# Products over partitions of an attention: from SBUF tiles into a PSUM bank of the logits, with a scan that restarts by a maximum

## The chip, the cores and the metric

The kernel runs on one core of one Trainium2 chip. The metric is the device time of one execution in microseconds (us); lower is better. The core has TensorE (PE in the profile, its weight loads PEld), VectorE (DVE), ScalarE (ACT), GpSimd (POOL), SyncE (SP, which here only issues transfers) and 16 DMA engines. Each engine runs its instructions in the order in which they stand in its queue.

## The reference

One layer of a hybrid encoder on `x` of 2048 x 1024 in float32: RMS norm, one input projection, three mixers side by side (a short gated convolution A, a convolution module B of width 31, and stick-breaking attention C with 8 heads of 64), one output projection, and a squared-ReLU MLP of width 4096, each with its residual, and a final RMS norm. The change is in the attention:

```python
z = jnp.einsum("bhqd,bhkd->bhqk", qb, kb) * scale
mask = s_idx < t_idx
log_beta = jax.nn.log_sigmoid(z)
log_1m = jnp.where(mask, log_beta - z, 0.0)
suffix = lax.cumsum(log_1m, axis=3, reverse=True) - log_1m
a = jnp.where(mask, jnp.exp(log_beta + suffix), 0.0)
out = jnp.einsum("bhqk,bhkd->bhqd", a, vb)
```

So the weight of key s for query t is sigmoid(z) times the product of (1 - sigmoid(z')) over all keys s' between s and t. The kernel forms that product directly.

## The kernel before

Keys lie on the 128 partitions, the 512 queries of a block in the free dimension. A key's partition p and step j say which key it is: of J keys that lie next to each other in time, each of the J steps takes one, so that a partition owns J successive keys. The product over later keys then falls into two: over the steps of the same partition, which is elementwise between tiles (`R`), and over the partitions behind it, which is the part that changes (`a_cross_a`).

`attention` runs over pairs (head h, query block i). For each pair `a_pass1` makes three diagonal steps (`a_diag`: logits `ps_z`, two sigmoids `om` and `A0` on ScalarE, masks on POOL at L537, products) and, for i > 0, 4i late steps. It carries the products over steps: for the diagonal in `om[:, hi2]` (L561 for 256 queries, L580 for the other 256), for the late steps in `R` (L603). The product over the 128 partitions goes so: each 32 x 32 block is transposed into a tile `T` of 16 groups x 33 columns (L564, L581 the two halves of the diagonal; L609 the late one); a scan from the right multiplies along the free dimension (L617), where the 33rd column of a group, set to 0 by POOL (L563, L608) and met by a 1 in the constant `d1`, begins each group anew; the products of whole groups of 32 partitions are chained in a small tile `C` (L620 or L622 the start, L625 three products of 32 x 16, L629 the total `tot`, which seeds the late part); the last product multiplies `T` by `C` (L631). `a_pass2` of the same pair, which runs interleaved with `a_pass1` of the next one, transposes the result back into a bank `ps_q` (L649), multiplies the `A0` tiles by it (L652, L659), splits each into a high and a low part (L88 on ScalarE, L90 on POOL) and multiplies by V (L697 to L706).

All of that runs beside a TensorE that is fed by other work: query block 0 beside the second half of the input projections (`p_half(1)`) and convolution B (L452 on VectorE); query blocks 1 to 3 beside the output projection and the FFN (`block`) of time blocks 0 to 2. `weave` hands out the attention steps in proportion to the main work. Instructions are then put in order by a scheduler that plays the program through with its own durations; on each engine the planned order is fixed. PSUM has eight banks: in the first part three for the projections (`ps_p`), one for convolution B, two for logits (`z`), one each for `ps_q` and `ps_o`; from the FFN on three for `ps_x`, `ps_u`, `ps_y`, three for logits, and the same two. Buffers of a tag are used in turn; whoever takes one waits for the last reader of the tile before. `om` has two buffers, `R` one in the first part and two later.

In the FFN, `fl` (L927) is the low part of an activation that TensorE multiplies next, and also frees the bank `ps_u`. L975 scales the eight tiles `acc` near the start of each block. In the first two blocks VectorE also splits the weights (`w<-wraw,w`, L90).

Of the kernel before, what the change touches and what calls it, by code (L numbers as in the profile page):

```python
# [15 lines left out]
P = 128  # L16
# [3 lines left out]
TB = 512  # L20
# [48 lines left out]
class Trunk:  # L69
# [126 lines left out]
    def attention_consts(self, ctx):  # L196
        nc = self.nc
        c = ctx.enter_context(self.tc.tile_pool(name="aconsts", bufs=1))
        self.d1 = c.tile([P, 16, 33], F32, name="d1")
        nc.vector.memset(self.d1, 0.0)  # L200
        nc.vector.memset(self.d1[:, :, 32:33], 1.0)


    def p_pools(self, ctx):
# [337 lines left out]
    def a_pass1(self, g):  # L542
        nc, pool, i = self.nc, self.at, g["i"]
        ab = self.ab
        lo, hi2 = slice(0, 256), slice(256, 512)

        def new(name, bufs, shape=(P, TB), dt=F32):
            return pool.tile(list(shape), dt, name=name, tag=name, bufs=bufs)

        if i:  # L550
            g["Kl"] = pool.tile([P, self.kmax], F32R, name="Kl", tag="Kl", bufs=self.ab["Kl"])
            for rows, kq in self.kq_halves(g["h"]):
                to = g["Kl"][rows, : TB * i].rearrange("c (j q) -> c j q", j=2)
                self.load_r(to, kq[:, 0, :, : TB * i // 2])
        A0 = g["A0"] = []

        k2 = [g["Kd"][:, 0:P], g["Kd"][:, 256 : 256 + P]]
        z = self.a_z(g, [(k2[1], lo, lo), (k2[0], lo, hi2)])
        t, om = self.a_diag(z, 0)
        nc.gpsimd.tensor_tensor(t[:, hi2], t[:, hi2], om[:, lo], op=ALU.mult)  # L560
        nc.vector.tensor_tensor(om[:, hi2], om[:, lo], om[:, hi2], op=ALU.mult)  # L561
        T = pool.tile([P, 16, 33], F32, name="T", tag="T1", bufs=ab["T1"])
        nc.gpsimd.memset(T[:, :, 32:33], 0.0)  # L563
        nc.vector.transpose(T[:, 0:8, 0:32], om[:, hi2])  # L564
        A0.append(t)
        yield 1

        k4 = self.every(g["Kd"], 4)
        z = self.a_z(g, [(k4[3], hi2, lo), (k4[2], hi2, hi2)])
        t, om = self.a_diag(z, 1)  # L570
        nc.gpsimd.tensor_tensor(t[:, hi2], t[:, hi2], om[:, lo], op=ALU.mult)
        R = new("R", ab["R"])
        nc.vector.tensor_tensor(R[:, lo], om[:, lo], om[:, hi2], op=ALU.mult)
        A0.append(t)
        yield 1
        z = self.a_z(g, [(k4[1], hi2, lo), (k4[0], hi2, hi2)])
        t, om = self.a_diag(z, 2)
        nc.vector.tensor_tensor(R[:, hi2], om[:, lo], R[:, lo], op=ALU.mult)
        nc.gpsimd.tensor_tensor(t, t, R, op=ALU.mult)
        nc.vector.tensor_tensor(om[:, hi2], om[:, hi2], R[:, hi2], op=ALU.mult)  # L580
        nc.vector.transpose(T[:, 8:16, 0:32], om[:, hi2])  # L581
        A0.append(t)
        yield 1
        tot = self.a_cross_a(g, T, None)
        if not i:
            return
        J = 4 * i
        kl = self.every(g["Kl"][:, : TB * i], J)
        full = slice(0, TB)
        R = None  # L590
        for j in range(J - 1, -1, -1):
            z = self.a_z(g, [(kl[j], full, full)])
            t = new("A0", ab["A0"])
            if R is None:
                nc.scalar.activation(t, z, AF.Sigmoid, scale=0.125)
                R = new("R", 2)
                nc.scalar.activation(R, z, AF.Sigmoid, scale=-0.125)
            else:
                nc.scalar.activation(t, z, AF.Sigmoid, scale=0.125)  # L599
                nc.scalar.activation(z, z, AF.Sigmoid, scale=-0.125)  # L600
                nc.gpsimd.tensor_tensor(t, t, R, op=ALU.mult)  # L601
                Rn = new("R", 2)
                nc.vector.tensor_tensor(Rn, z, R, op=ALU.mult)  # L603
                R = Rn
            A0.append(t)
            yield 1
        T = pool.tile([P, 16, 33], F32, name="T", tag="T2", bufs=1)
        nc.gpsimd.memset(T[:, :, 32:33], 0.0)  # L608
        nc.vector.transpose(T[:, :, 0:32], R)  # L609
        self.a_cross_a(g, T, tot)  # L610

    def a_cross_a(self, g, T, seed):


        nc = self.nc
        fl = lambda x: x.rearrange("p a b -> p (a b)")[:, ::-1]
        nc.vector.tensor_tensor_scan(fl(T), fl(T), fl(self.d1), 1.0, op0=ALU.mult, op1=ALU.add)  # L617
        C = self.tiny.tile([P, 16], F32, name="C", tag="C", bufs=3)
        if seed is None:
            nc.gpsimd.memset(C[96:128], 1.0)  # L620
        else:
            nc.vector.tensor_copy(C[96:128], seed)  # L622
        for a in (2, 1, 0):
            s, d = slice(32 * a + 32, 32 * a + 64), slice(32 * a, 32 * a + 32)
            nc.vector.tensor_tensor(C[d], C[s], T[s, :, 0], op=ALU.mult)  # L625
        tot = None
        if seed is None:
            tot = self.tiny.tile([32, 16], F32, name="tot", tag="tot", bufs=2)
            nc.vector.tensor_tensor(tot, C[0:32], T[0:32, :, 0], op=ALU.mult)  # L629
        qt = T[:, :, 1:33]  # L630
        nc.vector.tensor_tensor(qt, qt, C.unsqueeze(2).to_broadcast([P, 16, 32]), op=ALU.mult)  # L631
        g["qd" if seed is None else "ql"] = qt
        return tot

# [390 lines left out]
    def build(self):  # L1025
        tc = self.tc
        with ExitStack() as ctx:
            self.consts(ctx)
            self.attention_consts(ctx)
            self.raw = ctx.enter_context(tc.tile_pool(name="raw", bufs=1))  # L1030
            self.xb = 5
            self.presplit = [("w_out", c, q) for c in range(DC) for q in range(2)] + [("w1", c, q) for c in range(PRE) for q in range(2)]
            self.g, self.u, self.w, self.R, self.rv, self.sig, self.ca, self.ss, self.yraw = ({} for _ in range(9))
            with ExitStack() as c1:
                self.psum_pool(c1, d=3, c=1, z=2, q=1, o=1)
                self.p_pools(c1)
                self.w_eng = "dve"
                self.sb = 2
                self.xl = [[None] * DC for _ in range(2)]
                self.xh = [[None] * DC for _ in range(2)]  # L1040
                with tc.tile_pool(name="raw0", bufs=1) as self.rp:
                    self.rb, self.rt = 21, "raw"
                    self.p_start()
                self.rp = self.raw
                self.rb, self.rt = self.xb, "xt"
                self.at = c1.enter_context(tc.tile_pool(name="at1", bufs=1))
                self.ab = dict(Kl=1, A0=6, om=2, R=1, T1=2, Alo=2, Ahi=2, Vl=1, late=1, yc=2)
                weave(self.p_half(0), [(Side(self.mixer_b(0)), 83, 20, 225, True), (Side(self.x_norms()), 24, 60, 180, True)])
                self.heads = {}
                a0 = Side(self.attention([(h, 0) for h in range(H)]))  # L1050
                weave(self.p_half(1), [(Side(self.mixer_b(1)), 98, 0, 200, True), (a0, 28, 0, 210, True), (Side(self.pre_split()), len(self.presplit), 0, 200, True)])
            with ExitStack() as c2:
                self.psum_pool(c2, d=3, z=3, q=1, o=1)
                self.at = c2.enter_context(tc.tile_pool(name="at2", bufs=1, reuse_waits="tile"))
                self.st = c2.enter_context(tc.tile_pool(name="st2", bufs=1, reuse_waits="tile"))
                self.ha = c2.enter_context(tc.tile_pool(name="ha", bufs=1, reuse_waits="tile"))
                self.hp = c2.enter_context(tc.tile_pool(name="hp", bufs=1, reuse_waits="tile"))
                self.ob = 2
                self.kmax = 1536
                self.ab = dict(Kl=1, A0=15, om=2, R=2, T1=1, Alo=3, Ahi=3, Vl=2, late=2, yc=1)  # L1060
                at = Side(self.attention([(h, i) for i in (1, 2, 3) for h in range(H)]))
                self.heads = {}

                def attend(i):
                    while self.heads.get(i, 0) < H:
                        at.advance(at.done + 1)

                self.attend = attend
                self.end = iter(())
                for tb in range(4):  # L1070
                    weave(self.block(tb, self.end), [(at, (74, 95, 107)[tb], 45, 365 if tb < 2 else 320, False)] if tb < 3 else [])
# [48 lines left out]
```

## Time and profile before

| | |
|---|---|
| Median of 3 runs | 2449.74 us (2442.66 to 2449.86) |
| The profiled execution | 2452.1 us, its span 2450.4 us, mean granted TensorE clock 0.992 |
| Instructions in the span | 32556 |
| Scan L617, 56 times | 101.9 us of VectorE |
| Group products L625, 168 times | 90.0 us of VectorE |
| Last products L631, 56 times | 38.9 us of VectorE |
| Transposes L564, L581, L609, 88 times | 45.0 us of VectorE |
| Memsets L563, L608, L620, 88 times | 10.5 us of POOL |
| Conv B products L452, 240 times | 179.6 us of VectorE |

How to read it: a group line names the line of the kernel, the engine, the operation, what is written and read, shapes and count, then busy us, the mean in ns, and the idle time of the engine ahead of it with what ended it. A line of waits reads "engine tile line <- what it waited for: us in total, times, longest us". A line of windows names a stretch in us and the busy time of each engine in it. A line of the timeline starts with start and duration in us.

### The profile page before, as it was taken

The numbers are of one execution on the slowest core, as the hardware profiler recorded it, in microseconds if no ns is written. First come the engines' busy times: TensorE is split into PE (matmuls) and PEld (weight loads), VectorE is DVE, ScalarE is ACT, GpSimd is POOL, SyncE is SP. The second block draws the span as 40 slices with busy tenths as digits, with TensorE's granted clock in tenths as the row PEclk, the third lists the DMA queues.
The fourth block names the chain that finished last, engine by engine and source line by source line (L and its number), as shares of the span: only waits on it lengthen the run. The fifth ranks groups of instructions, "written<-read, shape, count | busy, mean of one in ns | idle before, by whom it ended". The sixth has DMA issues, their size and how long they took to land.

```text
span 2450.4 us, 32556 instructions
## 1 busy us (share of the span) xinstructions
PE 2390.6 (98%) x11316; PEld 2012.8 (82%) x11316; DVE 1620.1 (66%) x2380; ACT 1040.6 (42%) x1910; POOL 1161.3 (47%) x1221
## 2 busy tenths in 40 slices
PE   8999998999899999998999999999999999999998
PEld 7889877898788878887888888888888888888887
DVE  7957799943898977857777778577667735212114
ACT  5232532333466556534555555345555532121121
POOL 0342577641676666524676666168878720000000
PEclk9999999999999999999999999999999999999999
DMA  7569976779688777786877776876666556655555
GB/s 260 192 244 350 300 247 219 243 258 273 166 232 238 215 220 199 198 287 225 239 253 230 230 217 213 273 219 186 196 188 190 184 180 209 238 194 188 200 182 190
DMA packets 237061, 549.06 MB, mean 224 GB/s; under 512 B 26720, under 2 KB 100448, under 8 KB 218464
## 3 DMA queue, kind: packets, MB, share of 16 engines
q1 hardware_dynamic: 180304, 480.89, 58.1%
q0 software_dynamic: 37504, 56.64, 10.9%
q10 hardware_dynamic: 19088, 9.44, 1.3%
q8 instruction: 90, 1.47, 0.2%
q14 instruction: 75, 0.61, 0.1%
HBM read 390.38 MB, written 148.11 MB: 220 GB/s over the span
## 4 chain that ended last, share of the span: by engine, by line
PE 76%; DVE 15%; DMA 5%; issue 2%; POOL 1%; ACT 1%; SPq 0%; DVEq 0%; POOLq 0%; ACTq 0%
PE ps_y L107 8%; PE ps_y L103 8%; PE ps_y L105 8%; PE ps_u L103 7%; PE ps_u L105 7%; PE ps_u L107 7%; PE ps_p L105 4%; PE ps_p L107 4%; PE ps_p L103 4%; DVE A L659 2%; PE ps_x L103 2%; PE ps_z L518 2%; PE ps_x L105 2%; PE ps_x L107 2%; PE ps_z L519 2%
## 5 line engine op out<-in xcount | busy, mean ns | idle before, releaser
L90 POOL TENSOR_TENSOR Alo<-A,Ahi 128x512 fp32r<-128x512 f32 x288 | 395.1, 1383 | 104.2 <-PE ps_o L706 52.3
L952 DVE TENSOR_TENSOR acc<-acc,ps_y 128x512 f32<-128x512 f32 (+1 forms) x264 | 175.4, 667 | 195.6 <-PE ps_y L107 193.9
L107 PE MATMUL ps_y<-fl,w 128*128 128x512 f32 (+1 forms) x1056 | 279.8, 385 | 14.7 <-DVE fl L927 14.7
L103 PE MATMUL ps_u<-hh,w 128*128 128x512 f32 x1024 | 279.0, 393 | 6.2 <-DMA w<-s_w 6.2
L103 PE MATMUL ps_y<-fh,w 128*128 128x512 f32 (+1 forms) x1056 | 281.4, 386 | 2.5 <-DVE acc L952 1.3
L105 PE MATMUL ps_y<-fh,w 128*128 128x512 f32 (+1 forms) x1056 | 278.9, 384 | 0.0
L105 PE MATMUL ps_u<-hh,w 128*128 128x512 f32 x1024 | 275.0, 390 | 0.6 <-DVE w L90 0.6
L107 PE MATMUL ps_u<-hl,w 128*128 128x512 f32 x1024 | 275.0, 389 | 0.0
L601 POOL TENSOR_TENSOR A<-A,R 128x512 f32<-128x512 f32 x168 | 227.7, 1357 | 76.7 <-ACT A L599 54.6
L118 POOL TENSOR_TENSOR rs_y<-rs_v,mhalf 128x4 f32<-128x4 f32 (+1 forms) x13 | 14.7, 1131 | 523.3 <-DVE rs_v L117 486.1
L107 PEld LDWEIGHTS ps_y<-fl,w 128*128 128x128 f32 x1056 | 195.8, 189 | 55.9 <-DVE fl L927 17.0
L917 ACT ACTIVATE ps_u<-ps_u 128x512 f32<-128x512 f32 x128 | 74.8, 585 | 378.8 <-PE ps_u L107 378.5
L105 PEld LDWEIGHTS ps_y<-fh,w 128*128 128x128 f32 x1056 | 196.0, 189 | 40.2 <-DMA w<-wraw 0.4
L103 PEld LDWEIGHTS ps_y<-fh,w 128*128 128x128 f32 x1056 | 194.3, 189 | 40.7 <-DVE acc L952 2.1
L88 ACT ACTIVATE Ahi<-A 128x512 fp32r<-128x512 f32 x288 | 177.3, 627 | 118.4 <-PE ps_o L705 58.0
L105 PEld LDWEIGHTS ps_u<-hh,w 128*128 128x128 f32 x1024 | 192.1, 188 | 42.4 <-DVE w L90 1.5
L107 PEld LDWEIGHTS ps_u<-hl,w 128*128 128x128 f32 x1024 | 192.1, 188 | 40.1
L927 DVE TENSOR_TENSOR fl<-ps_u,fh 128x512 fp32r<-128x512 f32 x128 | 87.5, 685 | 207.1 <-ACT fh L926 206.6
L103 PEld LDWEIGHTS ps_u<-hh,w 128*128 128x128 f32 x1024 | 187.4, 189 | 42.5 <-DMA w<-s_w 6.4
L603 DVE TENSOR_TENSOR R<-ps_z,R 128x512 f32<-128x512 f32 x168 | 115.6, 688 | 126.4 <-ACT ps_z L600 93.8
L452 DVE SCALAR_TENSOR_TENSOR ps_c<-g,wb,ps_c 128x512 f32<-128x512 f32 x240 | 179.6, 748 | 4.6
L90 DVE TENSOR_TENSOR w<-wraw,w 128x512 fp32r<-128x512 f32 x152 | 150.4, 1007 | 24.1 <-ACT w L88 23.8
(175 smaller groups left out, 4881.2 us busy)
## 6 DMA issues: line engine op xcount, KB each, us to landing
w<-s_w SPq DMA_DIRECT2D x200, 512.0 KB, 3.4
w<-s_w SPq DMA_DIRECT2D x68, 1024.0 KB, 4.8
wraw<-in_w SPq DMA_DIRECT2D x192, 256.0 KB, 4.7
w<-s_w_out SPq DMA_DIRECT2D x64, 512.0 KB, 5.0
s_w<-w SPq DMA_DIRECT2D x32, 1024.0 KB, 5.4
s_w<-w SPq DMA_DIRECT2D x56, 512.0 KB, 4.4
Qd<-KQ SPq DMA_DIRECT2D x64, 256.0 KB, 6.4
xraw<-in_xT SPq DMA_DIRECT2D x48, 256.0 KB, 5.0
```

The source lines that it names most:

```text
L88: nc.scalar.activation(hi, x, AF.Copy)
L90: e.tensor_tensor(lo, x, f(hi), op=ALU.subtract)
L103: self.nc.tensor.matmul(ps, wh, xh, start=start and k == 0, stop=False)
L105: self.nc.tensor.matmul(ps, wl, xh, start=False, stop=False)
L107: self.nc.tensor.matmul(ps, wh, xl, start=False, stop=stop and k == n - 1)
L452: nc.vector.scalar_tensor_tensor(t, g[:, k : k + TB], self.wb[:, c, k : k + 1], t, op0=ALU.mult, op1=ALU.add)
L518: nc.tensor.matmul(z[:, oc], keys, g["qh"][:, qc], start=k == 0, stop=False)
L601: nc.gpsimd.tensor_tensor(t, t, R, op=ALU.mult)
L603: nc.vector.tensor_tensor(Rn, z, R, op=ALU.mult)
L917: nc.scalar.activation(ps, ps, AF.Relu)
L927: nc.vector.tensor_tensor(lo, ps, f(hi), op=ALU.subtract)
L952: nc.vector.tensor_tensor(acc[d][:, cols], acc[d][:, cols], ps, op=ALU.add)
```

## The change

The diagonal's products go to a tile of their own, `Rd` (from the tag `R`, which now has two buffers everywhere), in place of `om[:, hi2]`. `a_cross_a` takes `Rd` or `R` and does four things in another way. It transposes all 128 x 512 at once into a bank `X` from the logits' tag `z`. The scan reads `X` and writes `T` in SBUF; it first takes the maximum of the state and `d1` and then multiplies, so that a 1 in `d1` at the first column of a group (all products are at most 1) begins the group anew, and the columns are 32 apart without a gap. The group products are chained in `X[:, 0:16]` in place of `C`, whose start is set by VectorE in place of POOL. Then VectorE writes a 1 into the first column of the next group, so that `T[:, 1:513]` holds the exclusive products, and multiplies them by `C`. `T1` has one buffer everywhere. No matmul, transfer or ScalarE instruction is added or taken away.

```diff
-        self.d1 = c.tile([P, 16, 33], F32, name="d1")
+        self.d1 = c.tile([P, TB], F32, name="d1")
         nc.vector.memset(self.d1, 0.0)
-        nc.vector.memset(self.d1[:, :, 32:33], 1.0)
+        nc.vector.memset(self.d1[:, 31:TB:32], 1.0)
...
         nc.gpsimd.tensor_tensor(t[:, hi2], t[:, hi2], om[:, lo], op=ALU.mult)
-        nc.vector.tensor_tensor(om[:, hi2], om[:, lo], om[:, hi2], op=ALU.mult)
-        T = pool.tile([P, 16, 33], F32, name="T", tag="T1", bufs=ab["T1"])
-        nc.gpsimd.memset(T[:, :, 32:33], 0.0)
-        nc.vector.transpose(T[:, 0:8, 0:32], om[:, hi2])
+        Rd = new("R", 2)
+        nc.vector.tensor_tensor(Rd[:, lo], om[:, lo], om[:, hi2], op=ALU.mult)
...
-        R = new("R", ab["R"])
+        R = new("R", 2)
         nc.vector.tensor_tensor(R[:, lo], om[:, lo], om[:, hi2], op=ALU.mult)
...
-        nc.vector.tensor_tensor(om[:, hi2], om[:, hi2], R[:, hi2], op=ALU.mult)
-        nc.vector.transpose(T[:, 8:16, 0:32], om[:, hi2])
+        nc.vector.tensor_tensor(Rd[:, hi2], om[:, hi2], R[:, hi2], op=ALU.mult)
...
-        tot = self.a_cross_a(g, T, None)
+        tot = self.a_cross_a(g, Rd, None)
...
-        T = pool.tile([P, 16, 33], F32, name="T", tag="T2", bufs=1)
-        nc.gpsimd.memset(T[:, :, 32:33], 0.0)
-        nc.vector.transpose(T[:, :, 0:32], R)
-        self.a_cross_a(g, T, tot)
+        self.a_cross_a(g, R, tot)
...
-    def a_cross_a(self, g, T, seed):
+    def a_cross_a(self, g, R, seed):
...
-        fl = lambda x: x.rearrange("p a b -> p (a b)")[:, ::-1]
-        nc.vector.tensor_tensor_scan(fl(T), fl(T), fl(self.d1), 1.0, op0=ALU.mult, op1=ALU.add)
-        C = self.tiny.tile([P, 16], F32, name="C", tag="C", bufs=3)
+        X = self.ps.tile([P, TB], F32, name="ps_t", tag="z", bufs=self.banks["z"])
+        T = self.at.tile([P, TB + 1], F32, name="T", tag="T1" if seed is None else "T2", bufs=1)
+        nc.vector.transpose(X, R)
+
+        nc.vector.tensor_tensor_scan(T[:, 0:TB][:, ::-1], self.d1[:, ::-1], X[:, ::-1], 1.0, op0=ALU.max, op1=ALU.mult)
+        C = X[:, 0:16]
         if seed is None:
-            nc.gpsimd.memset(C[96:128], 1.0)
+            nc.vector.memset(C[96:128], 1.0)
         else:
             nc.vector.tensor_copy(C[96:128], seed)
+        first = T[:, 0:TB:32]
         for a in (2, 1, 0):
             s, d = slice(32 * a + 32, 32 * a + 64), slice(32 * a, 32 * a + 32)
-            nc.vector.tensor_tensor(C[d], C[s], T[s, :, 0], op=ALU.mult)
+            nc.vector.tensor_tensor(C[d], C[s], first[s], op=ALU.mult)
         tot = None
         if seed is None:
             tot = self.tiny.tile([32, 16], F32, name="tot", tag="tot", bufs=2)
-            nc.vector.tensor_tensor(tot, C[0:32], T[0:32, :, 0], op=ALU.mult)
-        qt = T[:, :, 1:33]
-        nc.vector.tensor_tensor(qt, qt, C.unsqueeze(2).to_broadcast([P, 16, 32]), op=ALU.mult)
+            nc.vector.tensor_tensor(tot, C[0:32], first[0:32], op=ALU.mult)
+        nc.vector.memset(T[:, 32 : TB + 1 : 32], 1.0)
+        qt = T[:, 1 : TB + 1]
+        q3 = qt.rearrange("p (a b) -> p a b", a=16)
+        nc.vector.tensor_tensor(q3, q3, C.unsqueeze(2).to_broadcast([P, 16, 32]), op=ALU.mult)
```

The order that the scheduler makes changes with it. Three places, of which the numbers behind a name are those of its buffer. First VectorE in the projections' second half, head 3 of query block 0; the rows begin with the half products of the third diagonal step. Before:

```order
L578 TENSOR_TENSOR R<-om,R 128x256
L580 TENSOR_TENSOR om<-om,R 128x256
L581 STREAM_TRANSPOSE T<-om 128x8x32
L617 SCALAR_TENSOR_TENSOR T<-T,d_90 128x528
L625 TENSOR_TENSOR C<-C,T 32x16 x3
L629 TENSOR_TENSOR tot<-C,T 32x16
L631 TENSOR_TENSOR T<-T,C 128x16x32
L649 STREAM_TRANSPOSE ps_q<-T 128x512
```

The same place with the change (the scan is L614, the group products are L623; `ps_t` is the bank X):

```order
L576 TENSOR_TENSOR R<-om,R 128x256
L578 TENSOR_TENSOR R<-om,R 128x256
L612 STREAM_TRANSPOSE ps_t<-R 128x512
L614 SCALAR_TENSOR_TENSOR T<-d_90,ps_t 128x512
L617 MEMSET ps_t 32x16
L623 TENSOR_TENSOR ps_t<-ps_t,T 32x16 x3
L627 TENSOR_TENSOR tot<-ps_t,T 32x16
L628 MEMSET T 128x16
L631 TENSOR_TENSOR T<-T,ps_t 128x512
L649 STREAM_TRANSPOSE ps_q<-T 128x512
```

Nothing else has moved in between; the two memsets are new on VectorE, and a part of the operands is now in the bank.

Second VectorE at the start of time block 1, where L975 scales `acc` while head 2 of query block 2 makes its diagonal. Before:

```order
L561 TENSOR_TENSOR om<-om 128x256
L975 TENSOR_TENSOR acc_10334<-acc_10334,ms 128x512
L975 TENSOR_TENSOR acc_10344<-acc_10344,ms 128x512
L975 TENSOR_TENSOR acc_10356<-acc_10356,ms 128x512
L975 TENSOR_TENSOR acc_10399<-acc_10399,ms 128x512
L975 TENSOR_TENSOR acc_10442<-acc_10442,ms 128x512
L564 STREAM_TRANSPOSE T<-om 128x8x32
L975 TENSOR_TENSOR acc_10485<-acc_10485,ms 128x512
```

And with the change, from the same step's product on and past the last two L975:

```order
L562 TENSOR_TENSOR R<-om 128x256
L975 TENSOR_TENSOR acc_10334<-acc_10334,ms 128x512
...
L975 TENSOR_TENSOR acc_10567<-acc_10567,ms 128x512
L927 TENSOR_TENSOR fl<-ps_u,fh 128x512
L571 TENSOR_TENSOR R<-om 128x256
L576 TENSOR_TENSOR R<-om,R 128x256
L578 TENSOR_TENSOR R<-om,R 128x256
L612 STREAM_TRANSPOSE ps_t<-R 128x512
```

The transpose that read `om` in the middle of the eight L975 is gone; the only one left reads `Rd` behind all of them.

Third TensorE at the same time: the four late logits tiles of that head. Before, they stand close together, with products by V between them:

```order
L518 MATMUL ps_z_10977<-Qd_9716,Kl_10785 128x512
L519 MATMUL ps_z_10977<-Qd_9716,Kl_10785 128x512
L518 MATMUL ps_z_11021<-Qd_9716,Kl_10785 128x512
L519 MATMUL ps_z_11021<-Qd_9716,Kl_10785 128x512
L705 MATMUL ps_o_10777<-Ahi_11031,Vl_10962 128x512
L706 MATMUL ps_o_10777<-Alo_11030,Vl_10962 128x512
L705 MATMUL ps_o_10777<-Ahi_11071,Vl_10962 128x512
L518 MATMUL ps_z_11061<-Qd_9716,Kl_10785 128x512
L519 MATMUL ps_z_11061<-Qd_9716,Kl_10785 128x512
L518 MATMUL ps_z_11091<-Qd_9716,Kl_10785 128x512
```

With the change the first row here ends the second late tile and the last begins the third:

```order
L519 MATMUL ps_z<-Qd,Kl 128x512
L705 MATMUL ps_o<-Ahi,Vl 128x512
L706 MATMUL ps_o<-Alo,Vl 128x512
L103 MATMUL ps_u<-hh,w_10830 128x512 x4
L105 MATMUL ps_u<-hh,w_10830 128x512 x4
L107 MATMUL ps_u<-hl,w_10830 128x512 x4
L103 MATMUL ps_u<-hh,w_10832 128x512 x4
L105 MATMUL ps_u<-hh,w_10832 128x512 x4
L107 MATMUL ps_u<-hl,w_10832 128x512 x4
L103 MATMUL ps_y<-fh,w_10691 128x512 x3
L518 MATMUL ps_z<-Qd,Kl 128x512
```

27 matmuls of the FFN now stand between the second and the third late tile. Three more runs of twelve (`w_10652`, `w_10720`, `w_10722`), which came behind all four tiles, now stand ahead of the first of them: 63 in all that have moved ahead of the third.

More of the change, by code (lines that the diff above doesn't have):

```diff
@@ L1046, in build @@
                 self.at = c1.enter_context(tc.tile_pool(name="at1", bufs=1))
-                self.ab = dict(Kl=1, A0=6, om=2, R=1, T1=2, Alo=2, Ahi=2, Vl=1, late=1, yc=2)
+                self.ab = dict(Kl=1, A0=6, om=2, Alo=2, Ahi=2, Vl=1, late=1, yc=2)
                 weave(self.p_half(0), [(Side(self.mixer_b(0)), 83, 20, 225, True), (Side(self.x_norms()), 24, 60, 180, True)])
@@ L1059, in build @@
                 self.kmax = 1536
-                self.ab = dict(Kl=1, A0=15, om=2, R=2, T1=1, Alo=3, Ahi=3, Vl=2, late=2, yc=1)
+                self.ab = dict(Kl=1, A0=15, om=2, Alo=3, Ahi=3, Vl=2, late=2, yc=1)
                 at = Side(self.attention([(h, i) for i in (1, 2, 3) for h in range(H)]))
```

## The prediction

> **What bounds the kernel now.** I read the page's busy line first, then the busy time by stage, then TensorE's waits. Stages are cut by what runs: 265 to 545 us is the second half of the projections with convolution B and attention of query block 0; 610 to 1090, 1090 to 1600 and 1600 to 2065 are the FFN of time blocks 0, 1 and 2, each with attention of the next block beside it.
>
> ```profile
> PE 2390.6 (98%) x11316; PEld 2012.8 (82%) x11316; DVE 1620.1 (66%) x2380; ACT 1040.6 (42%) x1910; POOL 1161.3 (47%) x1221
> ```
>
> ```profile
> 265.00:545.00 280.00, 268.60 (x1388) 228.62 (x1387) 230.98 (x340) 96.81 (x179) 191.67 (x206) 0.98 0.77 251
> 610.00:1090.00 480.00, 465.82 (x2139) 388.18 (x2139) 396.68 (x560) 273.24 (x508) 289.09 (x323) 0.99 0.75 216
> 1090.00:1600.00 510.00, 497.57 (x2275) 418.22 (x2274) 378.01 (x549) 262.62 (x485) 305.41 (x317) 0.99 0.76 241
> 1600.00:2065.00 465.00, 460.41 (x2087) 386.44 (x2086) 298.38 (x440) 223.18 (x407) 296.12 (x297) 1.00 0.62 188
> ```
>
> The columns behind the length are busy us of PE, PEld, DVE, ACT and POOL, then granted clock, DMA share and GB/s. TensorE is the bound, and the change takes no matmul away. So it can only win what TensorE loses in these stages: 11.4 + 14.2 + 12.4 + 4.6 = 42.6 us of idle time, and whatever clock the stops cost. Who ends them (total, times, longest):
>
> ```profile
> PE ps_y L107 <- DVE fl L927: 14.7, 6, 7.4
> ...
> PE ps_u L103 <- DMA w<-s_w: 6.2, 6, 1.8
> PE ps_z L518 <- ACT A L533: 5.9, 1, 5.9
> PE ps_mean L459 <- ACT cb L456: 4.1, 1, 4.1
> PE ps_ss L127 <- POOL sq L467: 3.1, 1, 3.1
> ...
> PE ps_z L518 <- DVE R L603: 1.7, 2, 1.1
> ```
>
> Most are a VectorE that lags behind the order the scheduler planned, either by itself (`fl`) or through ScalarE and POOL, whose instructions wait for it. Only the weight transfers have nothing to do with it. The clock behind two of the stops, those at 393 us (`ps_ss`) and 1117 us (`ps_z`):
>
> ```profile
> 394.00:404.00 10.00, 10.00 (x38) 8.37 (x39) 6.44 (x11) 1.73 (x5) 8.48 (x10) 0.70 0.43 128
> 1113.00:1121.00 8.00, 4.18 (x11) 3.16 (x12) 7.86 (x11) 5.32 (x11) 5.05 (x6) 0.57 0.50 155
> ```
>
> After the first, TensorE is busy throughout and yet has a clock of 0.70 for 10 us: 3.0 us more are lost. Around the second 0.43 of 8 us, 3.4 us, are lost. So a long stop costs its length plus about 3 us, and removing the whole of it returns both. For a stop that only becomes shorter I count no clock.
>
> **VectorE's side of it.** Some of its instructions wait inside their own duration (min/median/max ns):
>
> ```profile
> L625 DVE TENSOR_TENSOR C<-C,T x168: 172/181/4320, 291.7 to 1960.0; 32x16 f32<-32x16 f32 x168
> L617 DVE TENSOR_TENSOR_SCAN T<-T,d x56: 1236/1644/5677, 289.6 to 1955.5; 128x528 f32<-128x528 f32 x56
> L631 DVE TENSOR_TENSOR T<-T,C x56: 671/674/1124, 295.4 to 1960.3; 128x512 f32<-128x512 f32 x56
> ```
>
> ```profile
> L659 DVE TENSOR_TENSOR A<-A,ps_q x192: 647/680/690, 652.6 to 1968.8; 128x512 f32<-128x512 f32 x192
> ```
>
> The worst group of products, with what POOL did meanwhile (the first and last of three POOL products in a row):
>
> ```profile
> 380.89 5.65 DVE L625 TENSOR_TENSOR C<-C,T 32x16 f32<-32x16 f32 x3
> ```
>
> ```profile
> 382.50 1.29 POOL L90 TENSOR_TENSOR Alo<-A,Ahi 128x512 fp32r<-128x512 f32 x1
> ...
> 384.99 1.29 POOL L579 TENSOR_TENSOR A<-A,R 128x512 f32<-128x512 f32 x1
> ```
>
> `C<-C,T` has both inputs in SBUF; it takes 0.18 us or up to 4.3 us. The three stood until POOL's three were through: both end near 386.4. `A<-A,ps_q`, with one input in PSUM, never exceeds 690 ns in 192 runs beside the same POOL work. So what the change gives a PSUM input should lose these waits.
>
> **The change part by part: VectorE time.** Means from the groups:
>
> ```profile
> L617 DVE TENSOR_TENSOR_SCAN T<-T,d 128x528 f32<-128x528 f32 x56 | 101.9, 1819 | 1.1
> L625 DVE TENSOR_TENSOR C<-C,T 32x16 f32<-32x16 f32 x168 | 90.0, 536 | 5.6
> ```
>
> ```profile
> L649 DVE STREAM_TRANSPOSE ps_q<-T 128x512 f32<-128x512 f32 x56 | 40.0, 715 | 0.5
> ```
>
> ```profile
> L581 DVE STREAM_TRANSPOSE T<-om 128x256 f32<-128x256 f32 x32 | 14.1, 441 | 0.8
> ```
>
> ```profile
> L201 DVE MEMSET d<- 128x16 f32 x1 | 0.1, 72 | 0.1
> ```
>
> - Group products: 168 x (536 - 181) = 59.6 us less.
> - Scan: 512 elements at the floor's 1236/528 = 2.34 ns are 1.20 us; 56 x (1.82 - 1.20) = 34.7 us less. The trace shows no scan with a PSUM input or with a maximum as its first operation. Bounds: 1.82 us (nothing won) and 0.68 us (one pass, like `A<-A,ps_q`; 64 us won). I take the floor, the row nearest in kind.
> - Transposes: 64 halves at 0.44 us, 28.2 us, become 32 whole ones into PSUM at 0.715, 22.9: 5.3 us less. The late transpose only changes its place.
> - Added: 56 memsets of 16 columns in T and 32 in the bank at 0.072 us: 6.3 us more. The copy of the seed, `tot` and the last product T x C keep their size and get one PSUM operand: no change.
>
> Net 93 us of VectorE's 1620. [...]
>
> **POOL.** It loses 88 memsets of 0.1 us, and with them the waits ahead of them, since POOL stood in order behind a memset whose tile was still being read:
>
> ```profile
> POOL T L608 <- DVE ps_q L649: 54.2, 22, 7.4
> ...
> POOL T L563 <- DVE ps_q L649: 45.1, 21, 3.9
> ```
>
> Together 99 us of standing, after which POOL ran its backlog without a break, which is what locks VectorE out for microseconds. I expect shorter bursts but put no number on them: SBUF products that stay (`R<-om`, `w<-wraw,w`, `acc<-acc,ms`) still meet POOL.
>
> **What reaches TensorE**, stop by stop. Rows first:
>
> ```profile
> 1106.25 8.98 DVE L975 TENSOR_TENSOR acc<-acc,ms 128x512 f32<-128x512 f32 x5
> 1115.15 0.43 DVE L564 STREAM_TRANSPOSE T<-om 128x256 f32<-128x256 f32 x1
> ```
>
> ```profile
> 1115.68 0.60 ACT L532 ACTIVATE om<-ps_z 128x512 f32<-128x512 f32 x1 [5.88 <-DVE T L564]
> ```
>
> ```profile
> 622.67 1.06 DVE L625 TENSOR_TENSOR C<-C,T 32x16 f32<-32x16 f32 x1
> ```
>
> ```profile
> 265.00:394.00 129.00, 8.47 (x12) 0.97 0.83 278
> ```
>
> ```profile
> 2205.36:2266.62 61.26, 61.26 (x272) 50.70 (x272) 13.62 (x20) 7.05 (x12) 0.00 (x0) 1.00 0.53 188
> ```
>
> - 393 us, 3.1 + 3.0 us. Its chain runs back over VectorE without a gap to the 5.65 us above. Three products at 0.18 give 5.1 us back, more than the stop; the order around them stays. Gain 6.
> - 1117 us, 5.9 + 3.4 us. TensorE waits for ScalarE, which waits for a buffer of `om`, which L564 still reads, behind five L975. After the change the product into `Rd` is the last reader of both halves of that `om`, and it stands ahead of L975, so `om` is free 9 us sooner. Next late there is the new bank: the third late logits tile waits for the last product in it. L975 would end at 1117.8 (three more of 0.68 behind L564 and small change); two `fl`, three half products, transpose, scan, small ones and last product are some 6 us more, so 1124. TensorE, which stopped at 1110.9, has 63 FFN matmuls ahead of that tile in the new order, at 61.26/272 = 0.225 us (last row, no attention beside it) 14 us, so 1125. They are level; I leave a stop of 2 us. Gain 7.
> - 646 us (7.4 us, `fl` behind eight L975) and 378 us (4.1 us, convolution B on VectorE). Ahead of the first, one product took 1.06 us where 0.18 is needed. Ahead of the second, the 12 products up to 394 us took 8.47 us; without the 5.65 above, nine took 2.8 where 1.6 is needed. Gain 2.
> - The rest: 42.6 less 20.5 (these four) and the transfers' 6.2 is 16 us, short stops behind VectorE or POOL but for one of 4. If a fifth goes with VectorE's lag, 3 us.
> - New stops on the bank, next part: 2 us lost.
>
> 6 + 7 + 2 + 3 - 2 = 16 us. The profiled execution spans 2450.4 us and took 2452.1; the median of the runs shown is 2449.7, 2.4 below it. The forecast is for a median: 2449.7 - 16 = 2434.
>
> **The added wait.** The bank X is one of two (from 610 us on, three) that the logits use in turn, held from the transpose to the last product. Before, these two ends stood at:
>
> ```profile
> 349.20 0.43 DVE L581 STREAM_TRANSPOSE T<-om 128x256 f32<-128x256 f32 x1
> ...
> 355.68 0.67 DVE L631 TENSOR_TENSOR T<-T,C 128x512 f32<-128x512 f32 x1
> ```
>
> That is 7.2 us. Behind a waiting logits matmul stands all of TensorE, and behind that the ScalarE, VectorE and POOL work on its results. The scheduler answers by placing the matmul later: in the rows shown with the change, 27 matmuls, 6 us, now stand between that tile and the one ahead of it. Logits tiles that waited for VectorE before (`ps_z <- R`) stopped TensorE twice, 1.7 us in all; hence 2 us for 56 new cases.
>
> **Rivals.**
> 1. *Hidden anyway.* VectorE's relief is given back where it matters: the SBUF products that stay take over the waits for POOL (the five L975 above lost 8.98 - 5 x 0.68 = 5.6 us), so only one of the two big stops goes wholly and the other half. For it: those products carry most of the waiting that is left. Against: the 393 stop ends in group products alone. It gives about 9 - 5 = 4 us, 2446.
> 2. *Slower.* The plan knows no waits for POOL; where VectorE lags by more than the matmuls put ahead, TensorE stops on the bank. Price: a stop of 4 us (the long ones now are 3.1 to 7.4, the bank is held for 7.2) and 3 us of clock, 7 us each. Without the 2 us above 18 are won, so it decides from the third such stop; five cost 35 - 18 = 17 us: 2467. For it: VectorE is 83% busy in 610 to 1090 and lagged by 7.4 us at 646. Against: the matmuls put ahead.
> 3. *Larger.* With POOL's shorter bursts `fl` is no longer late either: the 14.7 us behind it go, less 1 counted, and twice 3 us of clock, since two of the six are long. 19 us more: 2415. For it speaks only that every long delay of VectorE is a wait with two SBUF inputs.
> 4. *It does not do what it says*: the waits are not for SBUF and stay. Against it stand the 192 runs of L659. It gives 2449.
>
> **How the numbers follow.** Forecast (2424 to 2442) 0.53, rival 3 0.13, rival 1 0.17, rival 2 0.14, rival 4 0.03. A measurement of this kernel can tell about 0.3%, 7.3 us, from no change. Faster than 2442.4: 0.53 + 0.13 less the edge, 0.64. Slower than 2457.1: 0.14. Within: 0.22. The range 2412 to 2456 takes in rivals 1, 3 and 4 and leaves out the greater part of rival 2. The scan's bounds move VectorE by +35 or -29 us; at the ratio above (16 of 93) that is some 5 us either way, inside it.
>
> **What would show it.** Right: group products at 0.18 us without a tail; the scan near 1.2 us; no POOL wait on T or C; VectorE near 1527 us; no stop of TensorE at `ps_ss` L127 near 390 us and none at `ps_z` behind ACT near 1115; `ps_z` waiting for the last product a few times, under 2 us. Wrong: products that still reach 1 us; several stops of 3 us and more at `ps_z` released by the last product; or a VectorE relieved by 93 us with TensorE's idle time unchanged.

## The result, and the profile after

| | before | after |
|---|---|---|
| Median, 6 runs each on one chip | 2448.76 us (2442.66 to 2455.13) | 2429.41 us (2425.46 to 2432.36) |
| Ratio | | 0.9912, 95% interval 0.9892 to 0.9933 |
| The profiled execution, its span | 2452.1, 2450.4 us | 2432.4, 2430.7 us |
| Mean granted clock | 0.992 | 0.994 |

The kernel is 19.3 us faster; 2434 was forecast. A profile shows one execution: those shown below of the first, third and sixth experiment ran 4, 7 and 9 us under the medians of their kernels. Busy time and the four stages of the changed kernel, in the columns of before:

```profile
PE 2387.3 (98%) x11316; PEld 2010.2 (83%) x11316; DVE 1545.9 (64%) x2436; ACT 1044.2 (43%) x1910; POOL 1128.9 (46%) x1133
```

```profile
265.00:545.00 280.00, 266.25 (x1352) 224.23 (x1351) 230.29 (x348) 96.30 (x178) 185.56 (x194) 0.98 0.75 246
610.00:1090.00 480.00, 472.50 (x2179) 393.56 (x2178) 375.92 (x584) 278.83 (x516) 281.28 (x298) 1.00 0.76 222
1090.00:1600.00 510.00, 504.48 (x2307) 424.00 (x2306) 356.89 (x573) 266.70 (x490) 298.13 (x292) 1.00 0.75 241
1600.00:2065.00 465.00, 464.87 (x2119) 392.40 (x2118) 280.81 (x460) 224.76 (x406) 285.57 (x277) 1.00 0.63 194
```

TensorE's idle time, length less busy time, is 13.8 + 7.5 + 5.5 + 0.1 = 26.9 us, where it was 42.6. The three FFN stages gained 6.7, 6.9 and 4.5 us; the first lost 2.4. The stages are cut at the same times as before. Of the span's 19.7 us, 16.4 are idle time that went (2450.4 - 2390.6 against 2430.7 - 2387.3), and 3.3 are matmuls that ran shorter, at a better clock (0.994 after 0.992).

VectorE's groups in the changed kernel, with busy us and mean ns behind the bar:

```profile
L614 DVE TENSOR_TENSOR_SCAN T<-d,ps_t 128x512 f32<-128x512 f32 x56 | 67.8, 1211 | 0.8
...
L578 DVE TENSOR_TENSOR R<-om,R 128x256 f32<-128x256 f32 x32 | 38.7, 1208 | 0.8
...
L576 DVE TENSOR_TENSOR R<-om,R 128x256 f32<-128x256 f32 x32 | 36.0, 1124 | 10.8 <-POOL om L537 10.6
...
L623 DVE TENSOR_TENSOR ps_t<-ps_t,T 32x16 f32<-32x16 f32 x168 | 30.8, 183 | 5.7
L571 DVE TENSOR_TENSOR R<-om 128x256 f32<-128x256 f32 x32 | 30.6, 957 | 7.0 <-POOL om L537 7.0
...
L562 DVE TENSOR_TENSOR R<-om 128x256 f32<-128x256 f32 x32 | 26.2, 820 | 3.0 <-POOL om L537 3.0
```

The same four half products of the diagonal before:

```profile
L580 DVE TENSOR_TENSOR om<-om,R 128x256 f32<-128x256 f32 x32 | 35.0, 1095 | 0.8
...
L578 DVE TENSOR_TENSOR R<-om,R 128x256 f32<-128x256 f32 x32 | 29.5, 923 | 8.1 <-POOL om L537 7.9
L573 DVE TENSOR_TENSOR R<-om 128x256 f32<-128x256 f32 x32 | 27.0, 844 | 5.4 <-POOL om L537 5.4
...
L561 DVE TENSOR_TENSOR om<-om 128x256 f32<-128x256 f32 x32 | 20.7, 648 | 5.1 <-POOL om L537 5.0
```

Group products and scan lost their tails at once: 90.0 - 30.8 = 59.2 us and 101.9 - 67.8 = 34.1 us. But the half products, whose two inputs stayed in SBUF, grew from 112.2 to 131.5 us. So VectorE as a whole lost 74.2 us, not 93. TensorE's waits after the change (total, times, longest):

```profile
PE ps_z L518 <- ACT A L533: 4.9, 2, 4.0
...
PE ps_z L518 <- DVE T L631: 3.5, 5, 1.1
PE ps_u L105 <- DVE w L90: 3.3, 1, 3.3
PE ps_mean L459 <- ACT cb L456: 2.2, 1, 2.2
...
PE ps_ss L127 <- POOL sq L467: 1.8, 1, 1.8
```

The 14.7 us behind `fl` are gone from the list, and so is the stop at 1117 us. The stops at 378 and 393 us became smaller (2.2 at 384, 1.8 at 398). New are 4.0 us at 330, 3.3 us at 896 (behind a weight split `w<-wraw,w`, again two SBUF inputs, that took 2.19 us) and 3.5 us on the bank of the new transposes. How the one at 330 us comes about shows best what happened in the first stage (start and duration in us; POOL, VectorE, ScalarE and TensorE in the order of time):

```profile
316.55 1.31 POOL L90 TENSOR_TENSOR Alo<-A,Ahi 128x512 fp32r<-128x512 f32 x1
...
317.12 4.78 DVE L578 TENSOR_TENSOR R<-om,R 128x256 f32<-128x256 f32 x1
...
320.32 1.28 POOL L577 TENSOR_TENSOR A<-A,R 128x512 f32<-128x512 f32 x1
...
326.77 0.69 DVE L342 TENSOR_TENSOR g<-ps_p,sig 128x512 f32<-128x512 f32 x1
...
327.56 0.23 ACT L343 ACTIVATE gt<-g 128x30 f32<-128x30 f32 x1 [10.92 <-DVE g L342]
...
330.13 0.39 PE L518 MATMUL ps_z<-Qd,Kd 128*128 128x256 f32 x1 [4.00 <-ACT A L533]
```

One half product stands for 4.78 us, until four POOL instructions in a row are through (the first and the last are shown); 0.42 would do. The gate `g` behind it on VectorE, which began at 320.9 us before, begins 5.9 us later, most of it from this product; ScalarE, which needs `g` first, stands for 10.9 us, and the sigmoids that free the logits' bank stand behind it. It is the same kind of wait as before, in another instruction. Whether the bank X has a part in this stop was not tested: from 322.5 to 332.4 us it holds one of the two logits banks, and the waiting tile has only the other.

### The profile page after: what moved, and what is told of

Its sections match the earlier page's. It is cut to its first block, busy times and chain, and to the rows that moved or that the text cites. A ratio compares the mean times of both kernels' runs of the same rounds, so it can differ in the third digit from the quotient of the medians.

```text
span 2430.7 us, 32476 instructions
## 1 busy us (share of the span) xinstructions
PE 2387.3 (98%) x11316; PEld 2010.2 (83%) x11316; DVE 1545.9 (64%) x2436; ACT 1044.2 (43%) x1910; POOL 1128.9 (46%) x1133
## 3 DMA queue, kind: packets, MB, share of 16 engines
q0 software_dynamic: 37504, 56.64, 10.9%
## 4 chain that ended last, share of the span: by engine, by line
PE 81%; DMA 7%; DVE 7%; issue 2%; POOL 1%; ACT 1%; SPq 1%; POOLq 0%; ACTq 0%; DVEq 0%
PE ps_y L107 9%; PE ps_y L103 9%; PE ps_y L105 9%; PE ps_u L103 9%; PE ps_u L105 9%; PE ps_u L107 9%; PE ps_p L107 3%; PE ps_p L105 3%; PE ps_z L518 2%; PE ps_z L519 2%; PE ps_p L103 2%; PE ps_x L103 2%; PE ps_x L105 2%; PE ps_x L107 2%; DMA w<-s_w 2%; DVE ps_c L452 2%
## 5 line engine op out<-in xcount | busy, mean ns | idle before, releaser
L90 POOL TENSOR_TENSOR Alo<-A,Ahi 128x512 fp32r<-128x512 f32 x288 | 385.5, 1348 | 136.6 <-ACT Ahi L88 70.4
L598 POOL TENSOR_TENSOR A<-A,R 128x512 f32<-128x512 f32 x168 | 221.9, 1323 | 135.7 <-ACT A L596 115.2
L118 POOL TENSOR_TENSOR rs_y<-rs_v,mhalf 128x4 f32<-128x4 f32 (+1 forms) x13 | 13.8, 1061 | 524.5 <-DVE rs_v L117 485.8
```

The costliest lines, as they stand in the source:

```text
L90: e.tensor_tensor(lo, x, f(hi), op=ALU.subtract)
```

## The experiments

Each ratio is to the kernel before on the same chip, with its 95% interval. "The three parts" are: group products in a bank; `Rd`, with `om` free sooner; transpose and scan on a bank.

**Group products alone, in the kernel before:**

```diff
-        C = self.tiny.tile([P, 16], F32, name="C", tag="C", bufs=3)
+        X = self.ps.tile([P, TB], F32, name="ps_t", tag="z", bufs=self.banks["z"])
+        C = X[:, 0:16]
...
-            nc.gpsimd.memset(C[96:128], 1.0)
+            nc.vector.memset(C[96:128], 1.0)
```

> The kernel before, with only the chain of group products (and the value that starts it) in a bank of the logits; transposes, scan, last product's T and `om` stay as before. Theory A (the waits of the group products carried most of the 19 us): the products fall from 536 to about 183 ns, VectorE loses some 60 us less what the half products take over, and the kernel gains 10 us or more (under 2440). Theory B (the gain needs the earlier release of `om` or POOL freed of its waits on T): VectorE loses the same 60 us, but the time moves by less than 5 us, and the stop at 1117 us behind ACT stays near 6 us.

Measured: 2437.75 against 2453.67 us, 0.9937 (0.9915 to 0.9960). Its groups of VectorE:

```profile
L617 DVE TENSOR_TENSOR_SCAN T<-T,d 128x528 f32<-128x528 f32 x56 | 108.2, 1933 | 1.0
...
L626 DVE TENSOR_TENSOR ps_t<-ps_t,T 32x16 f32<-32x16 f32 x168 | 30.8, 184 | 5.6
```

The products fall to 184 ns with transposes, scan and `om` as before, and theory A holds: by the medians this part alone gains 15.9 us, most of what the whole change does. The scan, still in SBUF, took 6 us of the waits over. The stop at 1117 us behind `om` is gone here too, without `Rd`. On the other side stands a stop on the new bank that the full change doesn't have, behind a half product that stands for 4.89 us (VectorE's and TensorE's timeline of this run):

```profile
346.37 4.89 DVE L580 TENSOR_TENSOR om<-om,R 128x256 f32<-128x256 f32 x1
...
358.45 0.58 PE L518 MATMUL ps_z<-Qd,Kd 128*128 128x256 f32 x1 [7.28 <-DVE T L632]
```

**The change without the group products:**

```diff
-        C = X[:, 0:16]
+        C = self.tiny.tile([P, 16], F32, name="C", tag="C", bufs=3)
```

> The changed kernel, with only the chain of group products taken back to the small SBUF tile; transpose and scan stay on the bank, which is free again after the scan. Theory A: the products are back near 0.5 us with a tail to some us, VectorE is 50 to 60 us longer than in the changed kernel, and 10 us or more of the 19 are lost (over 2439). Theory B: the time stays within 5 us of the changed kernel's 2429. The scan should stay at 1.21 us either way: it does not hang on the products.

Measured: 2447.43 us, 0.9975 (0.9959 to 0.9992). VectorE is back at 1613.0 us; the scan stays at 1213 ns. So the scan's relief does not hang on the products, and yet only 6 us of the 19 are left. Group products, and TensorE's wait on the bank:

```profile
L623 DVE TENSOR_TENSOR C<-C,T 32x16 f32<-32x16 f32 x168 | 90.0, 536 | 5.6
```

```profile
PE ps_z L518 <- DVE T L614: 14.6, 5, 5.1
```

Here VectorE lags and TensorE stops five times on the bank that the scan reads, three of them 3.2 to 5.1 us. These are the stops of the prediction's second rival, in a kernel that is still 6 us faster than before.

**`om` free sooner, alone, in the kernel before:**

```diff
-        nc.vector.tensor_tensor(om[:, hi2], om[:, lo], om[:, hi2], op=ALU.mult)
+        Rd = new("R", 2)
+        nc.vector.tensor_tensor(Rd[:, lo], om[:, lo], om[:, hi2], op=ALU.mult)
...
-        nc.vector.transpose(T[:, 0:8, 0:32], om[:, hi2])
+        nc.vector.transpose(T[:, 0:8, 0:32], Rd[:, lo])
```

and the same for the other half; T1 has one buffer.

> The kernel before, with only the diagonal's products in a tile `Rd` of their own, so that `om` is free sooner (and one T1 in the first part, for space). VectorE's busy time should stay within 10 us of before. Theory A: it removes the stop at 1117 us (5.9 us and 3.4 us of clock) and little else, so about 2442, 5 to 9 us gained. Theory B (release of `om` carries the gain): 12 us or more gained. If nothing is gained, the stop at 1117 us went with VectorE's lag and not with the release.

Measured: 2444.59 us, 0.9963 (0.9943 to 0.9982), 9.1 us by the medians. VectorE's 1614.5 us are nearly those of before, the stop at 1117 us is gone, and `fl` still costs TensorE 10.5 us in five stops. The gain is at the upper end of theory A's 5 to 9 us.

**The memsets of T and C on VectorE, in the kernel before:**

```diff
-        nc.gpsimd.memset(T[:, :, 32:33], 0.0)
+        nc.vector.memset(T[:, :, 32:33], 0.0)
```

and the same for the late T and for C.

> The kernel before, with its 88 memsets of T and C on VectorE in place of POOL, so that POOL never stands behind a T still in use (99 us of standing in before). Theory C (POOL's backlog after that standing is what locks VectorE out): VectorE falls by 20 us or more although it gets 88 small memsets (6 us) more, and the kernel gains 5 us or more. Theory A (the waits come from the products' two SBUF inputs, whenever POOL works): products and scan keep their means (0.54 and 1.82 us) within a tenth, and the time stays within 4 us of before.

Measured: 2468.09 us, 1.0061 (1.0043 to 1.0078): slower. POOL no longer stands behind T, and the waits of VectorE grew:

```profile
L617 DVE TENSOR_TENSOR_SCAN T<-T,d 128x528 f32<-128x528 f32 x56 | 111.7, 1995 | 1.0
L625 DVE TENSOR_TENSOR C<-C,T 32x16 f32<-32x16 f32 x168 | 103.5, 616 | 5.6
```

Theory C falls with the sign reversed, and theory A's "within a tenth" was missed as well. Taking POOL's standing away did not help; it may have kept POOL quiet while these products ran. That is a new theory, tested further down by putting the standing back into the changed kernel.

**The change again:**

> The changed kernel as it is, beside the next three on the same chip: ratio to before 0.989 to 0.993, like the first time (0.9912).

Measured: 2426.91 against 2450.35 us, 0.9915 (0.9892 to 0.9938), as at first. Its trace has much the same stops, but the one of `ps_ss`, 1.8 us at 398 in the first, is 0.6 us at 396 here, since the half product ahead of it took 1.43 us in place of 2.83, and the clock behind it stays at 1.00. The next three ran beside it.

**Group products and `Rd` together, without transpose and scan:** the edits of the first and third experiment in one.

> The kernel before with the two parts that gained alone, the group products in a bank (15.5 us) and `Rd` (9.1 us), without the transpose and scan on the bank; POOL still writes T's 33rd column. Theory D (the transpose and scan on the bank add nothing to the time, since their 34 us of VectorE go to the half products and to stops at `ps_z` L518): as fast as the changed kernel or up to 5 us faster, ratio to before 0.987 to 0.992, with the scan still near 1.9 us. Theory A (each part of VectorE's relief counts by its size): the scan's 34 us are missing, 5 to 8 us slower than the changed kernel, ratio 0.993 to 0.996.

Measured: 2438.15 us, 0.9948 (0.9929 to 0.9968). Not better than the group products alone (15.9 us there, 12.2 here, with overlapping intervals): the two gains don't add, and either of them alone removes the stop at 1117 us. Theory D's 0.987 to 0.992 was missed, and the ratio lies where theory A put it, 0.993 to 0.996. The full change is 11 us faster by the medians, but the intervals just overlap, and the profiles don't show what the 11 us would be: that of this run, of its fastest execution, is no longer than the changed kernel's (span 2427.9 against 2430.7 us). So it stays open whether the scan's relief, the transpose or the order of the full change counts. The longest stop here is that of the first experiment, and the scan has no part in it: ahead of it a half product takes 4.88 us, and the scan its floor of 1.24.

```profile
PE ps_z L518 <- DVE T L633: 9.4, 3, 7.3
```

**L975 from the bank, in the changed kernel:**

```diff
-        ms = hp.tile([P, TB], F32, name="ms", tag="ss", bufs=2)
-        nc.scalar.activation(ms, self.spread(mt, "z"), AF.Copy)
+        ms = self.spread(mt, "z")
```

> The changed kernel, in which the 32 products `acc<-acc,ms` (0.98 us, with a tail to 3.7) read the second operand from the bank that TensorE wrote, without ScalarE's copy to SBUF. If two SBUF inputs are what makes a product wait, they fall to about 0.68 us without a tail, 10 us less of VectorE. Time: theory A 0 to 3 us faster than the changed kernel; rival (the bank is now held for the eight products, some 6 us): a stop of 2 us or more at `ps_z` L518 or `ps_ss` behind L975 in some block, and no gain.

Measured: 2426.48 us, 0.9903 (0.9881 to 0.9925), not to be told from the change as it is. But the product behaves as said; 985 ns became

```profile
L974 DVE TENSOR_TENSOR acc<-acc,ps_R 128x512 f32<-128x512 f32 x32 | 19.6, 680 | 1.3 <-PE ps_R L134 1.3
```

That is a second kind of instruction in which one operand in PSUM takes the wait away, and no stop behind it is listed.

**The two products into `Rd` on POOL, in the changed kernel:**

```diff
-        nc.vector.tensor_tensor(Rd[:, lo], om[:, lo], om[:, hi2], op=ALU.mult)
+        nc.gpsimd.tensor_tensor(Rd[:, lo], om[:, lo], om[:, hi2], op=ALU.mult)
...
-        nc.vector.tensor_tensor(Rd[:, hi2], om[:, hi2], R[:, hi2], op=ALU.mult)
+        nc.gpsimd.tensor_tensor(Rd[:, hi2], om[:, hi2], R[:, hi2], op=ALU.mult)
```

> The changed kernel with the two half products into `Rd` (26.2 and 38.7 us of VectorE) on POOL, where a 128x256 product took 0.73 us. Theory C' (what the half products took over of the waits is what still limits VectorE): VectorE loses about 65 us, POOL gains about 47, and the kernel is 3 us or more faster than the changed one. Rival (POOL's longer stretches only move the waits to other SBUF products, and `Rd` comes later): VectorE loses under 50 us, the other half products and L90 get longer, time the same or slower.

Measured: 2422.35 us, 0.9889 (0.9866 to 0.9913), 4.6 us under the change by the medians; the intervals overlap. VectorE is at 1524.7 us, 23 less than in the changed kernel run beside it (1547.8), although 62 us of work left it. That half of the rival is true: the rows below, 151.4 and 30.4 us in the changed kernel, took over most of the 39 us. Its other half, a time that is the same or slower, was not seen, but the overlapping intervals don't exclude it.

```profile
L90 DVE TENSOR_TENSOR w<-wraw,w 128x512 fp32r<-128x512 f32 x152 | 158.1, 1059 | 32.7 <-ACT w L88 32.2
...
L571 DVE TENSOR_TENSOR R<-om 128x256 f32<-128x256 f32 x32 | 50.7, 1586 | 8.3 <-POOL om L537 8.3
```

**POOL stands behind T again, in the changed kernel:**

```diff
+        T = pool.tile([P, TB + 1], F32, name="T", tag="T1", bufs=1)
+        nc.gpsimd.memset(T[:, TB : TB + 1], 1.0)
         nc.vector.tensor_tensor(Rd[:, lo], om[:, lo], om[:, hi2], op=ALU.mult)
...
-        nc.vector.memset(T[:, 32 : TB + 1 : 32], 1.0)
+        nc.vector.memset(T[:, 32:TB:32], 1.0)
```

and the same for the late T.

> The changed kernel, in which POOL again writes one column of each T ahead of its use (the last one, which VectorE's memset then leaves out), at the places where before had its memsets of T. So POOL stands again until the transpose of the T before is done, and that is all that changes. Theory P (POOL's standing kept it quiet while VectorE made its products; without it the half products took the waits over): POOL waits on T some 80 to 110 us again, the four half products fall from about 130 us back to 112 to 118, and the time falls by 2 us or more, ratio to before under 0.990. Rival (the half products stand in the waits that scan and group products had, whatever POOL does): they stay at 126 us or more, and the time is the same or slower, 0.990 to 0.996.

Measured: 0.9897 (0.9882 to 0.9911), 2425.81 us. POOL's waits are back:

```profile
POOL T L563 <- DVE ps_q L652: 69.1, 26, 5.6
...
POOL T L607 <- DVE ps_q L652: 29.4, 15, 5.1
```

98.5 us of them, and the half products stay at 27.0 + 33.3 + 36.8 + 36.3 = 133.4 us. The ratio is a hair under the 0.990 that theory P asked for, but not to be told from the change's 0.9912 and 0.9915. Theory P falls by its mechanism: the half products took the waits over whether POOL stands or not. Why the kernel before became slower when POOL did not stand is not settled by this.

**Both edits, and all four half products on POOL:**

> The changed kernel with the two half products into `Rd` on POOL and L975 reading the bank, the two edits that gave 0.9889 and 0.9903 alone. If both relieve VectorE where it lags: VectorE near 1510 us, ratio 0.986 to 0.989. If the waits only move to L571, L576 and the weight split L90: VectorE 1520 us or more, ratio 0.989 to 0.992, no faster than the changed kernel.

> As the one before, with all four half products on POOL. VectorE then has hardly a product of two SBUF inputs left in the attention. If waits only move on, the weight split L90 (152 in the FFN, 1.0 us each, floor 0.67) gets longer by 15 us or more. If they go, VectorE falls under 1460 us. Time: 0.984 to 0.989 if VectorE's lag is what still costs; slower than the one before if POOL, which now makes the whole chain of the diagonal (about 47% to 52% busy), becomes what the logits wait for: then stops at `ps_z` or `ps_o` behind POOL of 2 us and more.

The first: 2411.43 us, 0.9833 (0.9816 to 0.9849), the fastest of all, and clear of the changed kernel's interval in both of its measurements. VectorE is where it was expected, near 1510 us, and the time is better than the 0.986 to 0.989 expected. The two edits alone gave 0.9889 and 0.9903; why they give more together was not isolated. The profile shows that the stops on the new bank, 7.0 us in the run with the two products on POOL, are down to 0.6. Its busy line, and TensorE's waits for others than transfers and the start:

```profile
PE 2378.8 (99%) x11316; PEld 2007.3 (83%) x11316; DVE 1509.8 (63%) x2372; ACT 1042.7 (43%) x1906; POOL 1166.3 (48%) x1197
```

```profile
PE ps_p L103 <- DVE u L355: 2.2, 1, 2.2
PE ps_y L103 <- DVE fl L927: 1.8, 2, 1.4
...
PE ps_mean L459 <- ACT cb L456: 1.2, 1, 1.2
```

The second: 2426.27 us, 0.9898 (0.9881 to 0.9916), slower than the first by 15 us although VectorE lost another 58:

```profile
PE 2383.4 (98%) x11316; PEld 2009.1 (83%) x11316; DVE 1451.5 (60%) x2308; ACT 1042.4 (43%) x1906; POOL 1216.7 (50%) x1261
```

```profile
L90 DVE TENSOR_TENSOR w<-wraw,w 128x512 fp32r<-128x512 f32 x152 | 180.3, 1204 | 39.5 <-ACT w L88 39.1
```

The weight split took 28 us of waits over (152.0 in the first). Stops behind POOL of 2 us, as expected for a slower kernel, don't show in its profile (1.3 us is the longest). TensorE's idle time is 6.0 us longer than in the first (2421.3 - 2383.4 against 2410.7 - 2378.8), and stops on the new bank are 3.8 of it (4.4 us against 0.6). The rest of the 15 us is open.

## Why the prediction was right, and where not

**VectorE.** Group products and scan were sized right (59.2 for 59.6, 34.1 for 34.7 us), and their mechanism is shown by the first two experiments and by L975 on the bank, whose mean of 985 ns became 680. The PSUM operand added no time to the small products: the median is 181 ns for the one that reads PSUM and 181 ns for the one from SBUF. The last product T x C nearly kept its size: its median went from 674 to 690 ns, its mean from 695 to 688. What the sum missed is the half products' 19.3 us more. The sum put nothing on the products that stay in SBUF. That they "take over the waits for POOL" was the first rival, and this half of it came true; the prediction had named `R<-om` as one that still meets POOL, but with no number.

**POOL.** "Shorter bursts" was the expectation. That POOL's standing and its backlog matter is not borne out: with the waits gone but the products in SBUF the kernel got slower (fourth experiment), and with the waits back in the changed kernel nothing moved.

**The stops.** The total, 16 us, was near the 19.3 measured, but the terms were not:
- *393 us*: 6 forecast; 1.3 gained in the first profiled execution, and in the second (the change again) 2.5 and the 3 us of clock, near the 6. In the first, the three group products do take 0.62 us, as argued, but the two half products ahead of them stand for 4.2 us longer than their floor of 0.42 each, and the clock behind the stop is as low as before (0.53 for 7 us). So the same kernel has this stop in two lengths, by how long the half products wait. Rows of the first execution, timeline and windows:

```profile
383.91 2.23 DVE L576 TENSOR_TENSOR R<-om,R 128x256 f32<-128x256 f32 x1
386.17 2.83 DVE L578 TENSOR_TENSOR R<-om,R 128x256 f32<-128x256 f32 x1
...
391.20 0.62 DVE L623 TENSOR_TENSOR ps_t<-ps_t,T 32x16 f32<-32x16 f32 x3
```

```profile
399.00:406.00 7.00, 7.00 (x20) 5.66 (x20) 5.04 (x6) 0.49 (x2) 6.34 (x8) 0.53 0.47 150
```

- *1117 us*: 7 forecast, and the 5.9 us stop is gone. The reason given, `om` released sooner, is enough by itself (third experiment), but so is VectorE's smaller lag (first experiment, where `om` was left as it was). Two causes were at hand for one stop, and they don't add. The stop's price was put too high: the window from 1113 to 1121 us, from which the prediction took 3.4 us of lost clock, holds 3.8 us in which TensorE stood. Behind the stop, from 1116.8 to 1121 us, the clock was 0.58, which loses 1.8.
- *646 and 378 us*: 2 forecast, too little. The first is gone with its 7.4 us and the one at 861 (4.2) with it; the one at 378 lost 1.9. The eight L975 ahead of the first, before and in the changed kernel:

```profile
632.08 12.27 DVE L975 TENSOR_TENSOR acc<-acc,ms 128x512 f32<-128x512 f32 x8
```

```profile
636.97 6.87 DVE L975 TENSOR_TENSOR acc<-acc,ms 128x512 f32<-128x512 f32 x8 [0.83 <-ACT ms L973]
```

  They met less of POOL in this place, which gives 5.4 us of the 7.4: POOL was busy for 11.0 of the 12.27 us, and is for 4.5 of the 6.87. That is the third rival's outcome for `fl`, with another cause than it named: with POOL's standing put back, `fl` is late no more either. Why just these products met POOL less was not isolated; the group products alone left 3.1 us of this stop, `Rd` alone 5.7, the change without the group products nothing.
- *The rest*: 3 forecast. The other four stops behind `fl`, some 3 us, went, but the new ones at 330 and 896 us, 7.3 us together, stand in no term of the sum.
- *New stops on the bank*: 2 forecast, 3.5 measured, the longest 1.1 us. The second rival's price (4 us and 3 us of clock each) was fair in the length: the variants that leave more waits on VectorE show such stops of 3.2 to 7.3 us. In the clock it was rather high for the changed kernel: behind its stops of 4.0 and 3.3 us, at 330 and 896 us, the clock was 0.56 for 3.9 us and 0.68 for 5.4 us, 1.7 us lost each. In the changed kernel no stop behind the last product is that long.

So the direction and the main mechanism were right, and the time was right partly by luck, with errors that cancel: the first stage's idle time did not fall (11.4 us before, 13.8 and 11.9 in the two profiled executions) where more than 6 us were counted, and the stops behind `fl`, of which little was counted, went almost entirely.

## What to carry to other kernels

When an instruction with two SBUF inputs waits for GpSimd, as the group products, the scan and L975 did here, a PSUM operand takes the wait from that instruction at once (means of 536, 1819 and 985 ns became 183, 1211 and 680), but part of it goes to the next instruction of that kind (the half products' 112.2 us became 131.5), so count the relief of the group and of its neighbours together. What VectorE saves is worth something only at the stops it causes: 74 us less gave 19 here, 58 us less in the last experiment gave a slower kernel. Two repairs of one stop don't add, while the two small edits that made the fastest kernel gave more together than each alone; test each alone and both. Profile the same kernel twice before you read a single stop: one of 1.8 us was 0.6 in the second execution.

## What the runs showed of the hardware that was not expected

- A waiting VectorE instruction can be passed by several GpSimd instructions in a row: the half product at 317 us stood through four of them, for 4.78 us.
- The waits are handed on even when work moves to GpSimd: 62 us of products taken from VectorE lightened it by 23.
- A scan with one PSUM input and a maximum as its first operation took 1193 to 1221 ns in its 56 instructions, per element close to the one that multiplies and adds from SBUF, when that doesn't wait (the median 1212/512 = 2.37 ns against the shortest 1236/528 = 2.34).
- The length of a stop of TensorE does not settle the clock behind it: 1.8 us at 398 us of the changed kernel were followed by 7 us at 0.53, as were the 3.1 us at 393 us before (6.9 us at 0.53), while behind 1.8 us at 1172 us before the clock was 1.00 (1172.27 to 1178 us).
